# Folded attention: two of a unit's four heads scaled on VectorE in one operation, two on ScalarE

## The chip, the cores and the metric

The kernel runs on one core of one Trainium2 chip. Time is device microseconds (us) of that core, given as the median of repeated executions. The engines are named as in the profile: PE is TensorE's matmuls, PEld its weight loads, DVE is VectorE, ACT is ScalarE, POOL is GpSimd, SP is SyncE, which issues most DMAs.

## The reference

A decoder block over 1024 tokens of width 1024, in float32: an RMSNorm, one combined projection, a retention branch, a sliding-window attention branch, a gated merge, and a SwiGLU feed-forward. The change lies in the attention branch alone. For each of 16 query heads of 64 channels and each block of 128 queries, with the keys of this block and the one before it and a learned sink per head:

```python
scores = jnp.einsum('bnqhgd,bnkhd->bnhgqk', qb, kb) * (d ** -0.5)
mask = (rel[None] >= 0) & (rel[None] < WINDOW) & (key_pos >= 0)
scores = jnp.where(mask, scores, -1e30)
m = jnp.maximum(jnp.max(scores, axis=-1, keepdims=True), sink)
e = jnp.exp(scores - m)
probs = e / (jnp.sum(e, axis=-1, keepdims=True) + jnp.exp(sink - m))
out = jnp.einsum('bnhgqk,bnkhd->bnqhgd', probs, vb)
```

## The kernel before

Matmul operands are split into a high part and a remainder (`h` and `l` in tile names), so that most products take three matmuls of 128x128 by 128x512.

The window is as long as a block. So for a query row each of the 128 key columns of a tile is valid in exactly one of the two key blocks: the scores of both blocks are folded into one 128x128 tile per head by a predicated copy, and the values are folded to match (`vev` holds even blocks, `vdf` differences).

The attention is cut into 32 units: unit u = 8g + b has the four heads of group g (0 to 3) and query block b (0 to 7). Its tiles: `sc` (128 queries x 4 heads x 132, two buffers) holds scores, then probabilities; column 128 holds the sink. `nm`, `den` and `rd` are 128x4: the negated maximum, the denominator, its reciprocal. The steps of a unit and their engines:

- `u_scores` (L462 to L498). POOL writes the sink column (L469). For each pair of heads PE makes the scores in a PSUM tile `s` (L477, L478), ACT copies one key block (L482), DVE puts in the other by the mask (L483) and reduces to `nm` (L485). In the first block of a group (b = 0) one DVE operation per head does this (L490). ACT takes the exponential of each head and its sum in `den` (L493, followed by an accumulator read). DVE takes the reciprocal of the four denominators (L496). ACT multiplies each head's 128x128 tile by its column of `rd`, in place: four instructions (L498).
- `u_transpose` (L500 to L518). PE transposes the four heads into one PSUM bank `pT` (L505); ACT casts it to `ph` (L507), DVE forms the remainder `pl` (L508) and, for b > 0, masked copies `qh` and `ql` (L515).
- `u_values` (L520 to L535). PE accumulates `pv` from `ph`, `pl`, `qh`, `ql` (L526). ACT and DVE add the two halves of the partitions in `tm` (L529 to L532) and write the result over the queries (L534, L535).

The loop at L555 emits for each i: `u_transpose(i-1)`, `u_scores(i)`, some steps of filling, `u_values(i-1)`. The filling (`Fill`, L189) is independent projection work: `quad_q` (L403) makes the queries of the next group, with ten DVE and four ACT operations of 128x512 in each half for bias, rotation and splitting (L427 to L446), and `gate` (L537) makes gate columns through `dense_g` and `mm_g` (L159 to L161). Their weights are split by ACT (L132, L419) and DVE (L135, L420).

The order in which the engines' instructions stand is not that of the code: a scheduler that puts independent instructions of the list between one another makes one fixed order for each engine when the program is built, and only blocks under `in_order` keep the written one. The attention loop is not under `in_order`. Each engine then runs its own list in order, and waits on semaphores for the others. All DMAs that the loop issues go through SP's queue, and none of them touches `sc` or `rd`.

After the attention come the retention's value product (L714), the other projections (L869), the retention core (L957), the branch outputs, and the feed-forward (L1545, L1847).

Of the kernel before, what the change touches and what calls it, by code (L numbers as in the profile page):

```python
# [15 lines left out]
ALU = mybir.AluOpType  # L16

P = 128
# [22 lines left out]
def hybrid_block(ctx: ExitStack, tc: tile.TileContext, x, ln1_g, w_in, b_in, ret_norm_g, w_ret_out,  # L41
                 attn_sinks, w_attn_out, w_out, ln2_g, w_gate, w_up, w_down, lnf_g,
                 c_ident, c_atab, c_rtab, c_amask, c_rmask, c_rcol, out):
    nc = tc.nc
    x = x[0]
    out = out[0]
# [23 lines left out]
    def ps(tag, bufs, name):  # L70
        return psum.tile([P, 512], F32, tag=tag, bufs=bufs, name=name)
# [231 lines left out]
    with tc.tile_pool(name="gt", bufs=1, side="right") as gt, tc.tile_pool(name="w1", bufs=1) as w1:  # L303
# [85 lines left out]
        for q in range(4):  # L389
# [4 lines left out]
            o = (q % 2) * 256  # L394
# [59 lines left out]
        def geo(u):  # L454
            g, b = divmod(u, NB)
            nk = 256 if b > 0 else P
            return g, b, nk, B[g // 2], (g % 2) * 4, slice(b * P, b * P + P)
# [4 lines left out]
        def u_scores(u):  # L462
            g, b, nk, Bt, jb, qc = geo(u)
            kv = g // 2
            k0 = (b - 1) * P if b > 0 else 0
            mk = amask[:, 0:P]
            sc = w1.tile([P, 4, 132], F32, tag="sc", bufs=2, name=f"sc{g}{b}")
            scs[u] = sc
            nc.gpsimd.tensor_copy(sc[:, :, P:P + 1], nsink[:, 4 * g:4 * g + 4].rearrange("p (j o) -> p j o", o=1))  # L469
            nm = tiny.tile([P, 4], F32, tag="nm", name=f"nm{g}{b}")  # L470
            den = tiny.tile([P, 4], F32, tag="den", name=f"den{g}{b}")
            for jp in range(2):
                pt = ps("s", 2, f"s{g}{b}{jp}")
                for jj in range(2):
                    j = 2 * jp + jj
                    o = pt[:, jj * 256:jj * 256 + nk]
                    nc.tensor.matmul(o, Bt[:, jb + j, qc], kst[:, kv, 0, k0:k0 + nk], start=True, stop=False)  # L477
                    nc.tensor.matmul(o, Bt[:, jb + j, qc], kst[:, kv, 1, k0:k0 + nk], start=False, stop=True)  # L478
                jr = slice(2 * jp, 2 * jp + 2)
                if b > 0:  # L480
                    ptv = pt.rearrange("p (j z s) -> p j z s", j=2, z=2)
                    nc.scalar.copy(sc[:, jr, 0:P], ptv[:, :, 1])  # L482
                    nc.vector.copy_predicated(sc[:, jr, 0:P], mk.bitcast(U32).rearrange("p (o s) -> p o s", o=1)  # L483
                                              .to_broadcast([P, 2, P]), ptv[:, :, 0])
                    nc.vector.tensor_reduce(out=nm[:, jr], in_=sc[:, jr, 0:P + 1], op=ALU.min,  # L485
                                            axis=mybir.AxisListType.X)
                for jj in range(2):
                    j = 2 * jp + jj
                    if b == 0:
                        nc.vector.tensor_tensor_reduce(out=sc[:, j, 0:P], in0=pt[:, jj * 256:jj * 256 + P], in1=mk,  # L490
                                                       scale=1.0, scalar=nsink[:, 4 * g + j:4 * g + j + 1],
                                                       op0=ALU.add, op1=ALU.min, accum_out=nm[:, j:j + 1])
                    nc.scalar.activation(sc[:, j, 0:P + 1], sc[:, j, 0:P + 1], AF.Exp, scale=-1.0,  # L493
                                         bias=nm[:, j:j + 1], accum_out=den[:, j:j + 1])
            rd = tiny.tile([P, 4], F32, tag="rd", name=f"rd{g}{b}")
            nc.vector.reciprocal(rd, den)  # L496
            for j in range(4):
                nc.scalar.activation(sc[:, j, 0:P], sc[:, j, 0:P], AF.Copy, scale=rd[:, j:j + 1])  # L498

        def u_transpose(u):  # L500
# [54 lines left out]
        for i in range(NU + 1):  # L555
            if i % NB == 0 and 0 < i < NU:
                fl.until(3 * (i // NB - 1) + 1)
            if i > 0:
                u_transpose(i - 1)
            if i < NU:  # L560
                u_scores(i)
            fl.step((i + 1) * left // (NU + 1) - i * left // (NU + 1))
            if i > 0:
                u_values(i - 1)
                if i % 4 == 0:
                    g, b, _, Bt, jb, _ = geo(i - 1)
                    c = slice((b // 4) * 512, (b // 4) * 512 + 512)
                    nc.sync.dma_start(ay_d[g, :, :, c], f32(Bt[:, jb:jb + 4, c]))
            if i == 2 * NB + 4:
                wv = act.tile([P, 16, 512], F32, tag="B", name="wv")  # L570
                for q in range(4):
                    nc.sync.dma_start(wv[:, 4 * q:4 * q + 4, :],
                                      w_in[(q // 2) * 512:(q // 2) * 512 + 512, C_RV + (q % 2) * 512:
                                           C_RV + (q % 2) * 512 + 512].rearrange("(k p) n -> p k n", p=P))
            if i > 3 * NB and i % 2:

                k = (i - 3 * NB) // 2
                nc.vector.tensor_tensor(out=wv[:, 4 + k, :], in0=wv[:, 12 + k, :], in1=wv[:, 4 + k, :],
                                        op=ALU.subtract)
# [1341 lines left out]
```

## Time and profile before

| what | value |
|---|---|
| median of 3 runs | 1569.12 us (1568.94 to 1569.2) |
| profiled execution: its own time | 1566.55 us |
| profiled execution: span of its instructions | 1564.8 us |
| mean granted clock of PE | 0.998 |
| four scales (L498) of a unit: first and last start over all units | 98.6 to 319.4 us |

The span runs from the first to the last recorded instruction; 1.75 us of the profiled execution's time lie around it. The attention units fill the stretch from about 98 to 326 us; the rest of the span contains none of them. In the views, a matmul's duration is longer than the interval at which matmuls follow one another, because they are pipelined, so PE can be busy nearly all the time and still be late; PEld's idle time before an instruction names what the weight load waited for. DVE and ACT instructions overlap a little too: the next one of a list may start before the last has ended.

### The profile page before, as it was taken

What the parts mean: (1) busy time and instruction counts of PE and PEld (TensorE: products, weight loads), DVE (VectorE), ACT (ScalarE), POOL (GpSimd) and SP (SyncE); (2) the same over time, 40 slices, a digit from 0 to 9 for tenths busy, and PEclk for the clock granted to TensorE, in tenths of its full rate; (3) what the DMA queues carried; (4) which work ended last, traced back from release to release, by engine and by line L of the source; (5) the groups of instructions that cost most, each with busy time, mean ns of one, the idle gap of its engine ahead of it and who ended that gap; (6) DMA issues with size and microseconds to landing.
All of it is one profiled execution on the core that took longest, in us unless ns stands there. A gap on an engine that the chain in (4) does not pass through costs nothing.

```text
span 1564.8 us, 20561 instructions
## 1 busy us (share of the span) xinstructions
PE 1549.0 (99%) x7323; PEld 1284.4 (82%) x7323; DVE 1016.2 (65%) x1668; ACT 735.2 (47%) x1556; POOL 375.3 (24%) x320
## 2 busy tenths in 40 slices
PE   9999999999999999999999999999999999999998
PEld 8887777788888888888888888888888888888886
DVE  6559878677667663877557789444444444678756
ACT  6358878834233333544224366333333333444445
POOL 2000000000055441000021124655555555100001
PEclk9999999999999999999999999999999999999999
DMA  6554655340464455654565402333333333862233
GB/s 219 168 160 123 208 209 162 129 134 35 154 204 149 138 165 189 227 193 150 175 195 190 167 1 88 121 102 102 108 103 109 105 101 102 289 255 90 92 102 127
DMA packets 152581, 228.43 MB, mean 146 GB/s; under 512 B 9307, under 2 KB 81821, under 8 KB 150942
## 3 DMA queue, kind: packets, MB, share of 16 engines
q1 hardware_dynamic: 152476, 227.10, 44.4%
q8 instruction: 58, 0.95, 0.2%
q14 instruction: 45, 0.37, 0.1%
q10 hardware_dynamic: 2, 0.00, 0.0%
HBM read 152.36 MB, written 69.99 MB: 142 GB/s over the span
## 4 chain that ended last, share of the span: by engine, by line
PE 88%; ACT 6%; DVE 4%; issue 1%; DMA 1%; SPq 0%; POOL 0%; POOLq 0%; ACTq 0%; DVEq 0%
PE fA L1545 15%; PE fB L1545 8%; PE dA L1847 7%; PE wA L869 7%; PE dxP L1847 6%; PE fC L1545 4%; PE wB L869 3%; PE wo L1379 3%; PE va L714 3%; PE woP L1379 2%; PE vP L714 2%; PE acc_ba L161 2%; PE acc_ba L159 2%; PE acc_ba L160 2%; PE acc_bb L159 2%; PE acc_bb L160 2%
## 5 line engine op out<-in xcount | busy, mean ns | idle before, releaser
L1847 PE MATMUL dA<-dwP,daP 128*128 128x512 f32 x528 | 120.6, 389 | 0.0
L1847 PEld LDWEIGHTS dA<-dwP,daP 128*128 128x128 f32 x528 | 99.0, 188 | 20.7 <-DVE dwP L135 0.2
L1847 PE MATMUL dxP<-dwP,daP 128*128 128x512 f32 x396 | 90.2, 389 | 0.0
L1847 PEld LDWEIGHTS dxP<-dwP,daP 128*128 128x128 f32 x396 | 74.3, 188 | 15.4
L159 PE MATMUL acc_g<-h,wh_g 128*128 128x512 f32 x192 | 76.9, 401 | 0.6 <-ACT wh_g L132 0.6
L469 POOL COPY sc<-nsink 128x4 f32<-128x4 f32 x32 | 11.2, 349 | 273.6 <-PE pT L505 237.2
L160 PE MATMUL acc_g<-h,wh_g 128*128 128x512 f32 x192 | 76.4, 398 | 0.0
L161 PE MATMUL acc_g<-h,wl_g 128*128 128x512 f32 x192 | 76.4, 399 | 0.0
L1620 POOL TENSOR_TENSOR xf<-xf 128x512 f32<-128x512 f32 x40 | 61.6, 1541 | 30.4 <-issue 28.8
L1551 POOL TENSOR_TENSOR xf<-xf 128x512 f32<-128x512 f32 x33 | 47.3, 1435 | 58.5 <-ACT xf L1553 26.9
L493 ACT ACTIVATE sc<-sc,nm 128x129 f32<-128x129 f32 x128 | 50.4, 397 | 19.3 <-DVE nm L485 15.4
L135 DVE TENSOR_TENSOR dwP<-wd,dwP 128x512 fp32r<-128x512 f32 x77 | 52.7, 684 | 4.6 <-ACT dwP L132 4.6
L1752 POOL TENSOR_TENSOR rs_f<-tot,mhalf 128x1 f32<-128x1 f32 x8 | 4.8, 606 | 205.4 <-DVE tot L1749 205.4
L132 ACT CAST daP<-daP 128x512 fp32r<-128x512 f32 x42 | 26.0, 621 | 55.0 <-PE dxP L1847 26.7
L132 ACT CAST dwP<-wd 128x512 fp32r<-128x512 f32 x77 | 47.4, 616 | 8.8 <-PE dA L1847 6.6
L159 PE MATMUL acc_bb<-ay,wh_bb 128*128 128x512 f32 x128 | 51.2, 400 | 0.0
L160 PE MATMUL aq<-h,wh_aq 128*128 128x512 f32 x128 | 50.6, 395 | 0.0
L161 PE MATMUL aq<-h,wl_aq 128*128 128x512 f32 x128 | 50.5, 395 | 0.0
L159 PE MATMUL aq<-h,wh_aq 128*128 128x512 f32 x128 | 50.3, 393 | 0.0
L160 PE MATMUL acc_bb<-ay,wh_bb 128*128 128x512 f32 x128 | 50.3, 393 | 0.0
L161 PE MATMUL acc_bb<-ay,wl_bb 128*128 128x512 f32 x128 | 50.1, 391 | 0.0
L159 PE MATMUL acc_ba<-yg,wh_ba 128*128 128x512 f32 x128 | 49.9, 390 | 0.0
(840 smaller groups left out, 4350.1 us busy)
## 6 DMA issues: line engine op xcount, KB each, us to landing
act_d<-xf SPq DMA_DIRECT2D x77, 256.0 KB, 2.0
daP<-act_d SPq DMA_DIRECT2D x21, 512.0 KB, 3.5
q_d<-stg SPq DMA_DIRECT2D x8, 1024.0 KB
q<-q_d SPq DMA_DIRECT2D x32, 256.0 KB, 6.0
ay_d<-q SPq DMA_DIRECT2D x8, 1024.0 KB
ay<-ay_d SPq DMA_DIRECT2D x4, 2048.0 KB, 14.3
wr_daP<-act_d SPq DMA_DIRECT2D x14, 512.0 KB, 6.8
wr_g<-in_w_in SPq DMA_DIRECT2D x12, 512.0 KB, 4.2
```

The costliest lines, as they stand in the source:

```text
L132: nc.scalar.copy(hi, raw)
L135: return nc.vector.tensor_tensor(out=lo, in0=raw, in1=f32(hi), op=ALU.subtract)
L159: nc.tensor.matmul(pt, hi[:, k, :], xh, start=(k == 0), stop=False)
L160: nc.tensor.matmul(pt, hi[:, k, :], xl, start=False, stop=False)
L161: nc.tensor.matmul(pt, lo[:, k, :], xh, start=False, stop=(k == 7))
L493: nc.scalar.activation(sc[:, j, 0:P + 1], sc[:, j, 0:P + 1], AF.Exp, scale=-1.0, bias=nm[:, j:j + 1], accum_out=den[:, j:j + 1])
L714: nc.tensor.matmul(vbanks[pr][tt], x_[:, c], w[:, u, :], start=(fresh and k + z == 0), stop=(k == 3 and z == 2), skip_group_check=not fresh)
L869: nc.tensor.matmul(pt, o[:, w, k, :], v, start=(first and k + z == 0), stop=(k == 3 and z == 2), skip_group_check=not first)
L1379: nc.tensor.matmul(bank, v[:, q + u, k, c], w[y][:, k % 2, :], start=(first and z == 0), stop=(last and z == 2), skip_group_check=not tracked)
L1545: nc.tensor.matmul(pt, o[:, w, k, :], v, start=(first and n == 0), stop=(n == 11), skip_group_check=not first)
L1620: nc.gpsimd.tensor_tensor(out=o, in0=a, in1=b, op=op)
L1847: nc.tensor.matmul(banks[tt], a[:, u, c], w[:, v, :], start=(fresh and f + z == 0), stop=(f == NP - 1 and z == 2), skip_group_check=not fresh)
```

## The change

Of the four scales of a unit, those of heads 0 and 1 become one DVE multiplication of a 128x2x128 part of `sc` by two columns of `rd`, each column repeated along the 128 keys by a stride of nothing. Heads 2 and 3 stay on ACT. Nothing else is edited.

```diff
             rd = tiny.tile([P, 4], F32, tag="rd", name=f"rd{g}{b}")
             nc.vector.reciprocal(rd, den)
-            for j in range(4):
+            nc.vector.tensor_tensor(out=sc[:, 0:2, 0:P], in0=sc[:, 0:2, 0:P],
+                                    in1=rd[:, 0:2].rearrange("p (j o) -> p j o", o=1).to_broadcast([P, 2, P]),
+                                    op=ALU.mult)
+            for j in (2, 3):
                 nc.scalar.activation(sc[:, j, 0:P], sc[:, j, 0:P], AF.Copy, scale=rd[:, j:j + 1])
```

## The prediction

> **What bounds the kernel now.** I read the page first, for how far PE is from full use and what its chain of waits names.
>
> ```profile
> span 1564.8 us, 20561 instructions
> PE 1549.0 (99%) x7323; PEld 1284.4 (82%) x7323; DVE 1016.2 (65%) x1668; ACT 735.2 (47%) x1556; POOL 375.3 (24%) x320
> ...
> PE 88%; ACT 6%; DVE 4%; issue 1%; DMA 1%; SPq 0%; POOL 0%; POOLq 0%; ACTq 0%; DVEq 0%
> ```
>
> The kernel is bound by PE: 88% of the chain is PE's, and only 10% belongs to ACT and DVE together. The change can earn no more than what PE loses in the attention. The view of stages shows how tight the helping engines are there (columns: length, then busy time of PE, PEld, DVE, ACT, POOL).
>
> ```profile
> 98.00:326.00 228.00, 221.63 (x1107) 177.59 (x1106) 184.06 (x419) 191.36 (x616) 10.40 (x30) 1.00 0.52 163
> ```
> ```profile
> 98.00:250.00 152.00, 147.62 (x740) 117.62 (x738) 131.41 (x298) 131.02 (x423) 8.32 (x21) 1.00 0.60 188
> 250.00:325.00 75.00, 73.02 (x365) 59.15 (x364) 51.84 (x120) 60.19 (x194) 2.07 (x9) 1.00 0.37 115
> 325.00:340.00 15.00, 15.00 (x68) 12.40 (x67) 14.13 (x14) 2.88 (x5) 0.00 (x0) 1.00 0.75 245
> ```
>
> ACT is busy for 84% of the attention (191.36 of 228) and DVE for 81%. Neither is full, but both are close enough to make PE late. Up to 250 us, where queries of the next group are made beside the units, they stand level at 86%; after that ACT has 80% and DVE 69%. The view of waits says who makes PE late (total, times, longest):
>
> ```profile
> DVE tm L531 <- ACT tm L530: 25.8, 23, 2.7
> ...
> PEld pT L505 <- ACT sc L498: 9.8, 31, 1.6
> ...
> ACT sc L498 <- DVE rd L496: 4.6, 9, 1.4
> ...
> PEld pv L526 <- ACT ph L507: 3.0, 6, 0.9
> ...
> PEld pv L526 <- DVE qh L515: 2.8, 6, 0.9
> PE pT L505 <- ACT sc L498: 2.1, 4, 1.2
> PE pv L526 <- DVE tm L532: 1.7, 3, 0.8
> ...
> PEld pv L526 <- DVE ql L515: 0.9, 4, 0.3
> ...
> PEld pv L526 <- DVE pl L508: 0.2, 1, 0.2
> ```
>
> The largest wait of PE's side is the one that the change touches: transposes that wait for ACT's scales, 9.8 us in 31 waits. Waits of `pv` for DVE's work come to 2.8 + 0.9 + 0.2 + 1.7 = 5.6 us in 14 waits. The first row matters for the cost: DVE itself stands idle before L531 in 23 of 32 units, 1.1 us each time.
>
> **The change part by part.** Removed: two of four ACT scales in each of 32 units. Added: 32 DVE multiplications of 128x256, placed after the reciprocal. No DMA, buffer or semaphore queue of SP or POOL is touched. The groups by shape have the scale itself and the nearest thing to the new operation, a DVE operation of 128x256 with both inputs in SBUF (L535, a subtraction):
>
> ```profile
> L535 DVE TENSOR_TENSOR q<-tm,q 128x256 fp32r<-128x256 f32 x31 | 12.9, 417 | 3.0 <-ACT q L534 3.0
> ```
> ```profile
> L498 ACT ACTIVATE sc<-sc,rd 128x128 f32<-128x128 f32 x128 | 40.9, 392 | 5.2 <-DVE rd L496 4.6
> ```
>
> Two stretches of the timeline show what these durations occupy. The first is the unit whose reciprocal starts at 253.77, one of a run of units that follow closely:
>
> ```profile
> 253.77 0.17 DVE L496 RECIPROCAL rd<-den 128x4 f32<-128x4 f32 x1
> 253.85 0.76 DVE L483 COPY_PREDICATED sc<-amask,s 128x256 f32<-128x256 uint32 x2
> 253.97 1.28 ACT L498 ACTIVATE sc<-sc,rd 128x128 f32<-128x128 f32 x4 [0.71 <-DVE rd L496]
> 254.50 0.74 DVE L485 TENSOR_REDUCE nm<-sc 128x2 f32<-128x258 f32 x2
> ...
> 256.06 0.42 DVE L531 TENSOR_TENSOR tm<-pv,tm 64x256 f32<-64x256 f32 x1 [0.82 <-ACT tm L530]
> ...
> 258.15 0.42 DVE L535 TENSOR_TENSOR q<-tm,q 128x256 fp32r<-128x256 f32 x1
> ...
> 258.48 0.69 DVE L515 TENSOR_TENSOR ql<-pl,amask 128x512 fp32r<-128x512 f32 x1
> ```
>
> Four scales last 1.28 us, one 0.39, so each after the first adds (1.28 - 0.39)/3 = 0.30. With two left the last scale ends 0.59 us earlier. On DVE, L535 lasts 0.42 but the next operation starts after 0.33. The new multiplication reads the result of the operation just ahead of it; where that happens in this trace, the second starts 0.03 after the first has ended:
>
> ```profile
> 767.18 0.69 DVE L1166 SCALAR_TENSOR_TENSOR ms<-tar,acc_ba 128x512 f32<-128x512 f32 x1 [4.19 <-DMA tar<-tb_d]
> 767.90 0.69 DVE L1167 TENSOR_TENSOR ms<-ms,mbr 128x512 f32<-128x512 f32 x1
> ```
>
> So it starts 0.17 + 0.03 = 0.20 after the reciprocal starts, ends at 0.62, and lets the next operation go at 0.53, where L483 now goes at 0.08: DVE's list is set back by 0.45 a unit. The trace has no operand repeated along its inner dimension by a stride of nothing; L515 and L483 repeat theirs along an outer one at no visible price. I take 0.42 and bound it by 0.33 and by 0.69, the time of an operation of twice the size.
>
> In this unit DVE would reach L531 at 255.24 + 0.45 = 255.69 and ACT would have `tm` ready at 256.06 - 0.59 = 255.47, so L531 starts 0.37 earlier than now. The idle 0.82 is the cover for the added DVE work. When the first transpose may go depends on ACT's list. Here ACT took its first scale as soon as `rd` came, ending 0.59 after the reciprocal's start; the DVE product ends at 0.62, 0.03 later. The second stretch shows the other kind, where ACT was still copying `tm`:
>
> ```profile
> 219.86 0.37 ACT L529 COPY tm<-pv 64x256 f32<-64x256 f32 x1
> 219.87 0.18 DVE L496 RECIPROCAL rd<-den 128x4 f32<-128x4 f32 x1 [0.27 <-ACT sc L493]
> ...
> 220.24 0.36 ACT L530 COPY tm<-pv 64x256 f32<-64x256 f32 x1
> ...
> 220.37 0.39 PE L159 MATMUL aq<-h,wh_aq 128*128 128x512 f32 x1
> 220.63 1.28 ACT L498 ACTIVATE sc<-sc,rd 128x128 f32<-128x128 f32 x4
> 220.64 0.42 DVE L531 TENSOR_TENSOR tm<-pv,tm 64x256 f32<-64x256 f32 x1 [0.59 <-ACT tm L530]
> ...
> 221.09 0.33 PE L505 MATMUL pT<-ident,sc 128*128 128x128 f32 x1 [0.33 <-ACT sc L498]
> ```
>
> `rd` is ready at 220.05, ACT starts scaling at 220.63 and PE idles until 221.09. The product would run from 220.08 to 220.50, in DVE's idle time. Nothing of DVE is late, and the wait is gone.
>
> The sum, against the profiled execution's 1566.55 us:
>
> - **A, transposes.** ACT waited for `rd` ahead of the scales only 9 times; in the other units it came late, as at 220. There the first transpose gains most of its wait; in the 9 only the later two gain. I take half of 9.8: -4.9 us. The bounds are 0 (the waits return at the next step) and -9.8.
> - **B, `ph`.** ACT's cast follows the transposes, but also stands behind other ACT work. Of the 3.0 us that `pv` waits for it I take a fifth: -0.6. The bounds are 0 and -3.0.
> - **C, DVE later by 0.45.** It is hidden in the 23 units with idle time before L531. In the other 9 of 32 (0.28) it is passed on to `qh`, `ql` or `tm`, where PE already waits 14 times: 14 x 0.45 x 0.28 = +1.8. If no cover held, 14 x 0.45 = +6.3. At best the freed ACT makes DVE's own inputs earlier and C is -1.
>
> Together -3.7 us: 1566.55 becomes 1562.85, and the median of 1569.12 becomes 1565.4. After the last unit PE goes on with work that does not depend on it (15.00 of 15 us busy at 325 to 340), so nothing further moves there. If A goes fully, the next late thing in the attention is `qh` from DVE.
>
> **The rivals.**
>
> 1. *The waits are PEld's and not PE's.* A weight load that waits 0.3 us may be hidden under a matmul still running: PE's own row has only 2.1 us in 4 waits. Then A is -2.1, B nothing, C +1.8: -0.3, so 1568.8. Against it: at 220.37 the matmul's successor comes 0.72 later, while only 0.33 of that is listed as PE's idle time, so PE's row understates the loss. The weight loads are busy 78% of the attention (177.59 of 228) and 83% in the dense stretch after it (12.40 of 15). The Trainium skill ("Perfetto Trace Analysis", section "Identifying the Most-Contended Engine") says to judge TensorE's room by weight-load time and not by matmul time, since pipelined matmuls mislead; by that rule PE's room here is an estimated 0.05 x 228 = 11 us, and not the 6 that its matmul row leaves, which speaks for A's larger bound.
> 2. *DVE becomes the bound, and it is slower.* Up to 250 us there are 22 reciprocals:
>
> ```profile
> L496 DVE RECIPROCAL rd<-den 128x4 f32<-128x4 f32 x22 | 3.8, 172 | 2.2 <-ACT sc L493 2.0
> ```
>
>    They take DVE from 131.4 to 141.3 of 152 us, 93%, while ACT falls to 131.0 - 22 x 0.59 = 118, 78%. Where the rotation of the queries runs beside a unit, DVE has no idle time between `rd` and `pl`, `qh`, `ql`, and each product is passed on to `pv`. It decides if the idle time before L531 is under 0.45 us in most of these units. Price: C in full, +6.3, and A only a quarter, -2.4: +3.9, so 1573.0. For it speaks the level load up to 250; against it the 23 idle times.
> 3. *The order changes.* PE's list here is not the code's (a projection matmul stands directly ahead of the transpose at 221.09). With one engine's work moved the scheduler may deal the filling out otherwise, and another wait opens or closes. Of this I can only say that it is of the size of the waits above, some 8 us either way: about 1561 or 1577.
>
> **How the numbers follow.** Chances: forecast 0.50, first rival 0.19, second 0.18, third 0.13. A run of this kernel can be told from no change at about 0.2%, which is 3.1 us. The forecast's -3.7 lies near that bound: of its 0.50 I put 0.38 beyond it and 0.12 within. The third rival is split 0.06 faster, 0.01 within, 0.06 slower. That gives faster 0.38 + 0.06 = 0.44, within 0.12 + 0.19 + 0.01 = 0.32, slower 0.18 + 0.06 = 0.24. The range runs from A in full with C at +1.8 and B at -0.6 (-8.6, 1560.5) to the second rival with one more microsecond for a product of 0.69 (1574.0).
>
> **What would show it.** Right: the wait of L505 for L498 falls by half or more; ACT's busy time between 98 and 326 falls by about 19 us (64 x 0.30) and DVE's rises by 11 to 14; the product lasts 0.42 and starts 0.03 after the reciprocal's end; DVE's idle time before L531 shrinks. Wrong: L505 waits for DVE instead, by as much; `pv` waits for `qh` and `ql` in more than 14 places; the product lasts 0.6 or more; or PE's list differs from before by more than the edit.

## The result and the profile after

The changed kernel takes 1563.65 us (median of 6 runs, 1562.86 to 1564.38) against 1569.03 before (6 runs, 1568.18 to 1569.2): 5.4 us less. The ratio is 0.9967 with a 95% interval of 0.9954 to 0.998, which is 3.1 to 7.2 us. The forecast was 1565.4, faster by 3.7.

First the page of the changed kernel: span, engines, and the chain that ended last.

```profile
span 1561.2 us, 20544 instructions
PE 1547.3 (99%) x7323; PEld 1284.1 (82%) x7323; DVE 1027.6 (66%) x1700; ACT 717.7 (46%) x1492; POOL 376.2 (24%) x320
...
PE 92%; ACT 3%; DVE 3%; issue 1%; DMA 1%; POOL 0%; SPq 0%; POOLq 0%; ACTq 0%; DVEq 0%
```

PE's share of the chain rises from 88 to 92%, and ACT's halves. The spans of the two traces differ by 3.6 us, less than the medians, because the profiled execution of before (1566.55) lay 2.6 us under its own median; the last section shows where such a difference can arise.

The stages of the attention, with the columns as before (length, then busy PE, PEld, DVE, ACT, POOL):

```profile
98.00:326.00 228.00, 223.58 (x1124) 180.36 (x1124) 198.70 (x456) 175.10 (x556) 10.57 (x30) 1.00 0.53 166
98.00:250.00 152.00, 148.50 (x756) 119.61 (x755) 140.51 (x324) 121.77 (x388) 9.05 (x22) 1.00 0.61 189
250.00:325.00 75.00, 74.08 (x365) 59.95 (x364) 57.23 (x132) 53.30 (x169) 1.52 (x8) 1.00 0.36 116
```

ACT's busy time falls by 16.3 us (191.36 to 175.10) and DVE's rises by 14.6 (184.06 to 198.70), so that now DVE is the fuller one: 92% up to 250 us. The waits in the attention (total, times, longest; L508 is the transpose, L529 `pv`, L534 the first addition of `tm`, L497 the product, L501 the two scales):

```profile
DVE tm L534 <- ACT tm L533: 11.5, 17, 1.6
...
PEld pv L529 <- ACT ph L510: 4.9, 13, 0.8
...
PEld pT L508 <- DVE sc L497: 2.6, 4, 1.5
PEld pT L508 <- ACT sc L501: 2.2, 9, 0.4
...
PEld pv L529 <- DVE pl L511: 1.5, 6, 0.5
...
PEld pv L529 <- DVE ql L518: 1.3, 6, 0.3
...
PEld pv L529 <- DVE qh L518: 0.7, 3, 0.3
```

The transposes waited 9.8 us for the scales and now wait 2.6 + 2.2 = 4.8 for product and scales together. DVE's idle time before the addition of `tm` falls from 25.8 to 11.5 us. The experiments ask which of the two rows marks the place of the gain.

The gain lies inside the attention. From the start of the first unit's reciprocal to that of the last it took 220.1 us before (98.0 to 318.1) and takes 216.6 now (98.5 to 315.1); from there to the end of the trace it is 1246.7 and 1246.1 us. So 3.5 of the 3.6 us between the two traces lie there.

### The profile page after: what moved, and what is told of

Its sections match the earlier page's. It is cut to its first block, busy times and chain, and to the rows that moved or that the text cites. A ratio compares the mean times of both kernels' runs of the same rounds, so it can differ in the third digit from the quotient of the medians.

```text
span 1561.2 us, 20544 instructions
## 1 busy us (share of the span) xinstructions
PE 1547.3 (99%) x7323; PEld 1284.1 (82%) x7323; DVE 1027.6 (66%) x1700; ACT 717.7 (46%) x1492; POOL 376.2 (24%) x320
## 4 chain that ended last, share of the span: by engine, by line
PE 92%; ACT 3%; DVE 3%; issue 1%; DMA 1%; POOL 0%; SPq 0%; POOLq 0%; ACTq 0%; DVEq 0%
PE fA L1548 15%; PE fB L1548 8%; PE dA L1850 7%; PE wA L872 7%; PE dxP L1850 6%; PE fC L1548 4%; PE wB L872 3%; PE wo L1382 3%; PE va L717 3%; PE acc_g L161 3%; PE acc_g L159 3%; PE acc_g L160 3%; PE woP L1382 2%; PE vP L717 2%; PE acc_ba L160 2%; PE acc_ba L159 2%
## 5 line engine op out<-in xcount | busy, mean ns | idle before, releaser
L469 POOL COPY sc<-nsink 128x4 f32<-128x4 f32 x32 | 11.3, 355 | 268.1 <-PE pT L508 207.8
L586 POOL TENSOR_TENSOR wr_wp<-wr_wp 128x512 f32<-128x512 f32 x10 | 16.5, 1653 | 140.2 <-DVE w0P L135 121.5
```

## The experiments

The scheduler makes a new order when one instruction is exchanged, so a changed kernel differs in two things: the work, and the order. To keep them apart, most experiments hold the lists of PE, DVE, ACT, POOL and SP, from the start to the end of the attention, to the order that the scheduler had made for the kernel before (or for the changed one). This is done by an ordering-only dependency from each instruction to the one ahead of it on its engine, which adds no wait on another engine:

```python
for i in todo:      # one engine's instructions in the wanted order
    if prev is not None:
        tc.add_manual_dep(i, prev.name, mybir.DependencyInfo(mybir.DependencyClass.NoSync,
                          mybir.DependencyReason.DATA), reason="pin")
    prev = i
```

No run holds the unchanged kernel to its own order. That the changed work gains as much with its order held (-5.5 us) as without (-5.2) speaks against a cost of the holding itself.

Each run was timed beside the kernel before on the same chip; three chips were used. The medians of before there were 1567.94 to 1568.56 us, so differences below are taken from the ratios, times 1568. The diffs are shortened: `(repeated)` stands for the columns repeated along the keys, `scratch` for a scratch tile (bfloat16 but for the run that says otherwise), and the lines that fix the order are left out.

**Work or order.** The changed work in the order of before, with the product directly behind the reciprocal:

```diff
-            for j in range(4):
+            nc.vector.tensor_tensor(out=sc[:, 0:2, 0:P], in0=sc[:, 0:2, 0:P], in1=rd[:, 0:2] (repeated), op=ALU.mult)
+            for j in (2, 3):
```

> The changed work in the order of before: every engine's list up to the end of the attention is held to the list of before, with the product directly behind each reciprocal and the two scales left on ACT where they stood. Theory W (the gain comes from the work that was moved: shorter wait of the transposes): 1563.5 to 1565.5 us, with L505's counterpart waiting about 5 us instead of 9.8. Theory O (the gain comes from the scheduler's other order): 1568 to 1571 us.

And the work of before in the order of the changed kernel:

> The work of before (four scales on ACT) in the order of the changed kernel; the two extra scales stand directly ahead of the two that ACT keeps there. Theory W: 1568 to 1571 us. Theory O: 1563 to 1565 us.

Measured: 1562.27 us, ratio 0.9965 (0.9953 to 0.9978), -5.5 us; and 1577.21 us, ratio 1.0058 (1.0045 to 1.0071), +9.1 us. The whole gain is there without the new order, so theory O falls. The new order is bad for the old work: the run is 6 us slower than the slowest that theory W allowed, so W is missed here too. Why the old work pays so much in that order is not shown. In that run's view of waits the transposes wait for four scales (L588) longer than they did before (9.8 us, 31 times):

```profile
PEld pT L595 <- ACT sc L588: 15.4, 65, 1.7
```

**Each half alone.** The scales of heads 0 and 1 left out, with nothing in their place (order of before):

```diff
-            for j in range(4):
+            for j in (2, 3):
```

> Order of before; heads 0 and 1 are left unscaled, so ACT has two scales less a unit and DVE nothing more. It measures the terms A and B without C. Theory W with my sizes (A -4.9, B -0.6): 1563.5 us. If C is worth +1.8 it is that much faster than the changed work in the same order; if C is nothing both are equal. Theory O: 1567 to 1569 us.

And a product that nothing needs added to the full work of before (order of before):

```diff
             nc.vector.reciprocal(rd, den)
+            nc.vector.tensor_tensor(out=scratch, in0=amask[:, 0:256], in1=rd[:, 0:2] (repeated), op=ALU.mult)
             for j in range(4):
```

> Order of before, all four scales on ACT, and behind each reciprocal a DVE product of 128x256 whose result nothing uses (written as bfloat16 to a scratch tile): it measures C alone. My C: +1.8, 1570.8 us. DVE bound (the second rival): +6.3, 1575.3 us. No cost: 1569 us.

Measured: 1558.63 us, ratio 0.9942 (0.9928 to 0.9955), -9.1 us; and 1568.38 us, ratio 1.0004 (0.9996 to 1.0013), +0.6 us with an interval across nothing. So the relief is worth 9.1 us by itself, well beyond the 5.5 that was expected (1563.5 us), and DVE's extra work costs next to nothing by itself. Yet both together give -5.5, so the product costs 3.6 us once ACT is relieved (1558.63 against 1562.27). The costs do not add. One thing the run without scales does not separate: its transposes of heads 0 and 1 need no reciprocal and no product at all, so part of the 3.6 could be probabilities that are ready later; the steps below speak for DVE's list. The waits of the run with the product alone show where most of it went (L630 is the first addition of `tm`):

```profile
DVE tm L630 <- ACT tm L629: 15.1, 18, 2.2
...
PEld pT L604 <- ACT sc L597: 9.0, 28, 1.4
```

DVE waited 25.8 us at this place and now 15.1: of the 32 x 0.45 = 14.4 us that the product adds, 10.7 went into idle time there. PE's wait for the scales is about what it was.

**Earlier probabilities or a shorter list on ACT.** The change does two things to ACT: the probabilities are complete 0.59 us sooner, and ACT is free 0.59 us sooner for what stands behind. Two useless scales behind the two real ones keep the first and take away the second (order of before, product on DVE; `scratch` is one float32 tile here):

```diff
+            for j in (0, 1):
+                nc.scalar.activation(scratch, amask[:, 128 * j:128 * j + 128], AF.Copy, scale=rd[:, j:j + 1])
```

> Order of before, product on DVE, and ACT keeps four scales: first the two real ones of heads 2 and 3, then two on other data whose result nothing uses. ACT's list is as long as before; only the time at which the probabilities are ready is earlier (by 0.59 us for the last one). If the gain is the earlier transposes: 1562 to 1564 us. If it is ACT's shorter list (copies, exponentials and casts coming earlier): 1566 to 1569 us.

Measured: 1572.16 us, ratio 1.0024 (1.0013 to 1.0035), +3.8 us: worse than either theory. The cause was in the experiment. Both useless scales write the same tile, and the second seems to have waited for the first; the timeline has the four together from 136.69 to 138.09, where four took 1.28:

```profile
136.69 0.68 ACT L596 ACTIVATE sc<-sc,rd 128x128 f32<-128x128 f32 x2
137.27 0.82 ACT L598 ACTIVATE scratch_a<-amask,rd 128x128 f32<-128x128 f32 x2
138.11 0.37 ACT L629 COPY tm<-pv 64x256 f32<-64x256 f32 x1
```

ACT was thus held about 0.13 us longer in each of 32 units, 4.2 us in all, and the kernel became 3.8 us slower. The error measures how directly ACT's list sets the time: in 21 of the 31 steps from one unit's reciprocal to the next, the trace has 0.12 to 0.15 us more than that of before. With a place of its own for each of them (and bfloat16):

> As the run with ACT's load kept, but the two useless scales write to tiles of their own (bfloat16), so that the second need not wait for the first: there the four took 1.42 us a unit instead of 1.28, and all that followed came 0.13 us a unit later. Theory of ACT's list (what matters is how long ACT is held, not when the probabilities are ready): as with the product alone, 1568 to 1570 us. If the earlier probabilities help beside it: 1564 to 1567 us.

Measured: 1568.13 us, ratio 1.0003 (0.9994 to 1.0012). All of the change's gain is gone, though the probabilities are ready as soon after the reciprocal as with the change, and 21 of the 31 steps last as long as before within 0.03 us. PE's listed wait for the scales (L596) has shrunk to 3.0 us, and 2.4 more lie at the transposes for ACT work ahead of the scales (L630); that earned nothing:

```profile
DVE tm L631 <- ACT tm L630: 16.2, 19, 2.2
...
PEld pv L626 <- ACT sc L590: 3.3, 6, 1.2
PEld pT L605 <- ACT sc L596: 3.0, 11, 0.6
PEld pT L605 <- ACT tm L630: 2.4, 4, 1.0
```

So earlier probabilities alone win nothing; the time hangs on how long ACT is held. The traces suggest a loop that ACT and DVE run between each other. In the run with the changed work in the old order it reads so (rows of DVE and ACT alone; L588 reciprocal, L589 product, L591 scales, L622 and L623 copies of `tm`, L577 reduction, L624 addition of `tm`); it is the unit that the prediction quotes from 253.77 on:

```profile
254.38 0.17 DVE L588 RECIPROCAL rd<-den 128x4 f32<-128x4 f32 x1
254.58 0.42 DVE L589 TENSOR_TENSOR sc<-sc,rd 128x256 f32<-128x256 f32 x1
254.58 0.70 ACT L591 ACTIVATE sc<-sc,rd 128x128 f32<-128x128 f32 x2 [0.76 <-DVE rd L588]
254.92 0.77 DVE L575 COPY_PREDICATED sc<-amask,s 128x256 f32<-128x256 uint32 x2
255.30 0.37 ACT L622 COPY tm<-pv 64x256 f32<-64x256 f32 x1
255.59 0.74 DVE L577 TENSOR_REDUCE nm<-sc 128x2 f32<-128x258 f32 x2
255.69 0.36 ACT L623 COPY tm<-pv 64x256 f32<-64x256 f32 x1
...
256.25 0.41 DVE L624 TENSOR_TENSOR tm<-pv,tm 64x256 f32<-64x256 f32 x1
...
259.27 0.17 DVE L588 RECIPROCAL rd<-den 128x4 f32<-128x4 f32 x1
...
259.48 0.69 ACT L591 ACTIVATE sc<-sc,rd 128x128 f32<-128x128 f32 x2 [0.77 <-DVE rd L588]
```

The addition of `tm` needs ACT's copies, which stand behind the scales, and it stands behind the product and the next unit's reduction on DVE. It starts 1.87 us after the reciprocal, where it was 2.29 (253.77 to 256.06). Behind it DVE runs without a gap to the next reciprocal (3.02 us, before 3.03), and that releases ACT's next scales, which wait 0.77 for it. Before, ACT was the late one at the addition, by 0.82; now DVE is, and `tm` has lain ready since 256.05. The next reciprocal comes after 4.89 us. Before, it came after 5.32:

```profile
253.77 0.17 DVE L496 RECIPROCAL rd<-den 128x4 f32<-128x4 f32 x1
...
259.09 0.17 DVE L496 RECIPROCAL rd<-den 128x4 f32<-128x4 f32 x1
```

**How many heads, and which.** If that loop is the limit, moving k heads shortens ACT's way to the addition by 0.30 k and lengthens DVE's; the gain ends where DVE is later. All in the order of before:

> Order of before; DVE scales head 0 alone (128x128), ACT three heads. ACT's list is 0.30 us a unit shorter, half of the change's. Theory of ACT's list: half of what dropping two scales gave is -4.6, less the product's cost of 1 to 3: -2 to -3.5 us against before, 1565 to 1567. If the gain needs the whole pair: no change.

> Order of before; DVE scales all four heads in one product of 128x512, ACT none. DVE is set back by some 0.7 us a unit, 23 us in all, against 25.8 us that it waits before its addition of tm; ACT is relieved of 1.2 us a unit. If DVE's idle time covers it: 1560 to 1563 us. If DVE is full: 1566 us or more.

> Order of before; DVE takes heads 2 and 3, ACT heads 0 and 1, while PE still transposes 0 to 3 in turn. The last probabilities are ready as early as with the change, the first wait for ACT's list again. If the first transpose's wait for ACT's list is the gain (as at 220 us in the trace of before): 1565 to 1568 us. If the end of the four scales is the gain: 1562 to 1563.5 us.

Measured: one head 1561.94 us, ratio 0.9967 (0.9955 to 0.998), -5.2 us; four heads 1568.53, ratio 1.0008 (0.9999 to 1.0017), +1.3 us; heads 2 and 3 in place of 0 and 1, 1566.02, ratio 0.9983 (0.9975 to 0.9992), -2.7 us. One head earns as much as two, where I had expected about half. Four heads earn nothing, as the second of the two theories had it: DVE is nearly full, busy for 142.82 of the 152 us up to 250. The choice of heads falls between its two theories. The wait before the addition of `tm` runs down with the dose: 25.8 us with no head, then with one (L626) and with four (L619); with two it is 9.4 in the same order:

```profile
DVE tm L626 <- ACT tm L625: 13.6, 20, 2.1
```
```profile
DVE tm L619 <- ACT tm L618: 4.1, 7, 1.4
```

The table puts the loop's arithmetic beside the runs. For each case it has the time from the reciprocal to the addition of `tm` in the unit at 254 us: DVE is ready 1.47 after the reciprocal before (255.24 - 253.77) and ACT 2.29. A 128x128 product lasts 0.29 in the run with one head, so it sets DVE back by some 0.32, one of 128x256 by 0.45, and one of 128x512 by 0.72. "This step" is the change of the time from this unit's reciprocal to the next one's, as that run's trace has it; nothing in it is fitted. The column "by the loop" scales the change of the later one by the run without two scales (-9.1 us for -0.59), which is therefore no test.

| case | ACT ready | DVE ready | addition moves | this step, us | by the loop, us | measured, us (95%) |
|---|---|---|---|---|---|---|
| product added alone | 2.29 | 1.92 | 0 | +0.01 | 0 | +0.6 (-0.6 to +2.0) |
| ACT's load kept, second version | 2.29 | 1.92 | 0 | -0.01 | 0 | +0.5 (-0.9 to +1.9) |
| one head on DVE | 1.99 | 1.79 | -0.30 | -0.30 | -4.6 | -5.2 (-7.1 to -3.1) |
| two heads (the change) | 1.70 | 1.92 | -0.37 | -0.43 | -5.7 | -5.5 (-7.4 to -3.4) |
| four heads | 1.10 | 2.19 | -0.10 | -0.17 | -1.5 | +1.3 (-0.2 to +2.7) |
| two scales left out | 1.70 | 1.47 | -0.59 | -0.57 | -9.1 | -9.1 (-11.3 to -7.1) |

The step that took 5.32 us before, in the traces without two scales, with one head and with four:

```profile
248.69 0.17 DVE L586 RECIPROCAL rd<-den 128x4 f32<-128x4 f32 x1
253.44 0.17 DVE L586 RECIPROCAL rd<-den 128x4 f32<-128x4 f32 x1
```
```profile
251.54 0.17 DVE L590 RECIPROCAL rd<-den 128x4 f32<-128x4 f32 x1
256.56 0.17 DVE L590 RECIPROCAL rd<-den 128x4 f32<-128x4 f32 x1
```
```profile
256.46 0.17 DVE L585 RECIPROCAL rd<-den 128x4 f32<-128x4 f32 x1
261.61 0.17 DVE L585 RECIPROCAL rd<-den 128x4 f32<-128x4 f32 x1
```

In this unit the loop's arithmetic holds to within 0.07 us in all six runs. But this unit is not the mean of all: 31 steps of -0.43 would be 13 us, and the changed work gains 4.2 over them (220.1 us to 215.9). The steps differ, and set side by side the traces without two scales (211.3 us) and with the changed work (215.9), both in the order of before, show where the product costs its 4.6 us (3.6 between the timed medians). In 18 of the 31 steps it costs 0.07 or less. In nine it costs 0.28 to 0.59 each, 3.7 in all: those that begin, in the trace of before, at 116.58, 133.38, 138.70, 155.63, 165.16, 227.63, 236.80, 248.93 and 309.79. In six of the nine DVE had been idle there for at most 0.1 us ahead of any addition of `tm`, so there was no idle time that could take up the product. The step from 227.63 is one of them: before, without two scales, and with the changed work it takes 9.17, 8.73 and 9.16 us.

```profile
227.63 0.17 DVE L496 RECIPROCAL rd<-den 128x4 f32<-128x4 f32 x1
236.80 0.18 DVE L496 RECIPROCAL rd<-den 128x4 f32<-128x4 f32 x1
```
```profile
223.36 0.17 DVE L586 RECIPROCAL rd<-den 128x4 f32<-128x4 f32 x1
232.09 0.17 DVE L586 RECIPROCAL rd<-den 128x4 f32<-128x4 f32 x1
```
```profile
227.65 0.17 DVE L588 RECIPROCAL rd<-den 128x4 f32<-128x4 f32 x1
236.81 0.17 DVE L588 RECIPROCAL rd<-den 128x4 f32<-128x4 f32 x1
```

I made the table's sum after the runs, so it is an argument and not a forecast that came true. Scaled up from one unit it misses four heads by more than the interval: the step at 254 is 0.17 shorter there, but the one from 248.93 grows from 4.84 to 5.59. And it knows nothing of the choice of heads: with heads 2 and 3 on DVE the loop is the same, but 2.8 us of the gain are lost (the two intervals just overlap). So beside a shorter list on ACT it does count which probabilities are ready first. There PE waits 7.1 us for ACT's scales of the heads that it transposes first (L591), against 2.4 us in 8 waits with the changed work in the same order:

```profile
PEld pT L598 <- ACT sc L591: 7.1, 19, 1.3
```

**Further relief for ACT.** If ACT's list is the limit, POOL might take some of it, as it is nearly idle there. One head on POOL, two on DVE, one on ACT, first in the order of before, then in one of the scheduler's own; and the changed kernel with the cast of a unit's result on POOL:

```diff
+            nc.gpsimd.tensor_tensor(out=sc[:, 3, 0:P], in0=sc[:, 3, 0:P], in1=rd[:, 3:4] (repeated), op=ALU.mult)
```
```diff
-            nc.scalar.copy(v[:, :, 0, :], tm)
+            nc.gpsimd.tensor_copy(v[:, :, 0, :], tm)
```

> Order of before on PE, DVE, ACT and SP: heads 0 and 1 on DVE, head 2 on ACT, head 3 on POOL, which is nearly idle in the attention. ACT has three scales less. If the shorter list of ACT is worth more than POOL's slower product costs: 1560 to 1562 us. If head 3 comes late from POOL: 1563 us or more, with the transposes waiting for POOL.

> The changed kernel with head 3 on POOL and one scale left on ACT, in an order of its own (before it stood in the order of before). Theory of ACT's list: -1 to -4 us against the changed kernel, 1560 to 1563. If POOL's product is too slow for the transposes: 1564 or more.

> The changed kernel, in an order of its own, and besides the cast of each unit's result to its high part goes from ACT to POOL (128x256, SBUF to SBUF): another 0.30 us a unit off ACT's list and nothing on DVE's. Theory of ACT's list: another -2 to -4 us, 1559 to 1562. If ACT is no longer what holds PE after the change, or if DVE's subtraction behind the cast waits for POOL: 1563 to 1566.

Measured: 1563.53 us, ratio 0.9973 (0.9963 to 0.9983); 1567.79, ratio 0.9992 (0.9982 to 1.0002); 1564.2, ratio 0.9978 (0.9969 to 0.9987). None beats the change: more relief for ACT is not turned into time. The reason is argued and not shown. It fits the unit at 254, in which DVE is the later one with two heads. But ACT is not out of the way everywhere: with the cast on POOL, DVE still waits 11.3 us for ACT's copies of `tm`, 17 times (11.5 us, 17 times, with the change). The first of the three lies where its second theory put it, but not for the reason given: its view of waits has no row of transposes that wait for POOL. POOL's product lasts 0.64 us, where ACT's lasts 0.39. Why POOL's head costs so much more in the scheduler's own order was not followed up; that kernel's runs spread from 1563.1 to 1568.9 us, so its median says little, and in its trace the products are longer, 0.49 us on DVE and 0.68 on POOL, against 0.42 and 0.64 in the order of before.

## Why the prediction was right, and where its steps were not

- **What bounds the kernel**: right. The gain came from PE's lost time in the attention. The room of an estimated 11 us, which the Trainium skill's rule in "Perfetto Trace Analysis", section "Identifying the Most-Contended Engine", gave from the weight loads, agrees with the runs: leaving two scales out won 9.1 us, more than the 6 that the matmul row leaves and far more than the 2.1 of PE's own wait row. The first rival, 1568.8 us, falls.
- **The durations**: right. The product lasts 0.42 us, also with an operand repeated by a stride of nothing, and starts 0.03 after the reciprocal ends (254.58) where it stands directly behind it; the next operation follows 0.34 later. In the unit at 254 us the addition of `tm` came 0.42 earlier, by forecast 0.37.
- **Terms A and B, -5.5 together**: right in sign, too small, and for another reason than was given. The relief alone is worth -9.1. The wait row of A moved as forecast (9.8 to 4.8), but it is a mark of ACT's lateness and not the place of the gain: with ACT's load kept the row fell also, and the time did not. Both ways that the prediction names, the first transposes that no longer wait for a late ACT (as at 220) and the last scale that ends 0.59 us earlier, are kept in that run, and alone they earned nothing. What earned was that ACT comes free 0.59 us sooner for the copies, casts and exponentials behind the scales. The run with the other two heads suggests that the first transposes add to it once ACT is relieved. B rose instead of falling in the changed kernel: `pv` waits 4.9 us for `ph` there, 3.0 before; in the order of before it fell, to 1.6.
- **Term C, +1.8**: right in sign, too small. Alone the added DVE work costs +0.6 (-0.6 to +2.0), beside the relief 3.6. "It is hidden in the 23 units with idle time before L531" held in the main: in 18 of 31 steps the product costs 0.07 us or less. The failing step is the sizing of the rest, "14 x 0.45 x 0.28": it let the product count only where `pv` already waited for DVE. The traces show it passed on in nine steps, by 0.41 us on average of the 0.45, 3.7 us in all. And A and C are not separate, as I reckoned them: in the unit at 254 they share the same 0.82 us, and from 227.63 on the product takes back 0.43 of the 0.44 us that the relief won.
- **Luck in the number**: -9.1 + 3.6 = -5.5 was forecast as -5.5 + 1.8 = -3.7. The gain and the cost were both put too low by the same kind of step, reading them from PE's wait rows, and the two errors half cancel. The range held; the forecast's mechanism held in part.
- **Second rival, DVE as the bound**: it did not decide with two heads, but its mechanism is seen in the nine steps, most of which had no idle time on DVE. With four heads, 0.72 us a unit in place of 0.45, all of the gain is gone. The point from which it decides lies between.
- **Third rival, the order**: the order did change within the attention, which the prediction had named as a sign of being wrong. For the changed work it made no difference that can be measured: -5.5 in the old order, -5.2 in the new. For the old work it did, +9.1 us, which is of the size that this rival gave. Order and work belong together, and that the new order would fit the new work so well was not foreseen.
- **The signs to look for**: the wait of L505 fell by half, as said, and `pv` waits for `qh` and `ql` in 9 places, not in more than 14. ACT's busy time fell by 16.3 and not by 19 in the window from 98 to 326; the scales themselves fell from 40.9 to 22.2 us, so other work of ACT has probably moved into the window. DVE's rise, 14.6, is a little over the 11 to 14 given.

## What to carry to other kernels

Where two helper engines release each other in a loop, an engine's idle time is not a free reserve beside the other's lateness: both can be the same interval, and moving work can win at most the point where the two ways meet. So work out both ways to the meeting instruction and take the later one, rather than adding a gain on one engine to a cost on the other. Do it for each kind of unit: here the unit at 254 alone says that four heads gain a little, and the units without idle time on DVE pay so much that nothing is left. The longest wait of the bound engine shows which engine is late, but whether the gain is made there is told only by a run that keeps the wait short and the load long.

## What the runs showed of the hardware

The start of the kernel comes in two versions. The first transposes of the first normalization (count, durations, then first and last start) began at 7.2 to 7.6 us in eleven of the fourteen traces and at 9.5 in the other three: that of the changed work in the old order, the first one with ACT's load kept, and the one with POOL's head in an order of its own. The order up to there is held to that of before in the first two of them, and also in seven traces that start early. Here are before and the changed work in the old order:

```profile
L221 PE MATMUL lnT<-ident,wk x64: 270/273/463, 7.2 to 36.3; 128*128 128x128 f32 x64
```
```profile
L313 PE MATMUL lnT<-ident,wk x64: 270/273/421, 9.5 to 38.7; 128*128 128x128 f32 x64
```

The 2.3 us are carried through to the attention (the last of these transposes is 2.4 later, the first reciprocal 2.5). They are nearly half of the effect studied here, which a single pair of traces could hide or double: the traces of before and of this run have spans of 1564.8 and 1562.6, 2.2 us apart, where the timed runs differ by 5.5. Each kernel was traced once, so that one kernel shows both versions is likely and not shown; the traced execution of this run was the slowest of its five (1564.46 us, the others 1561.74 to 1563.29). Runs of the kernel before scatter over 3 to 4 us on one chip (1566.2 to 1570.3 on all three), and only repeated runs settle such a difference. What delays the start was not traced to its cause.
